# A weight pool allocated ahead of a small pool: the same program with one group of tiles at another on-chip address

## The chip, the cores and the metric

One NeuronCore of one Trainium2 chip runs the whole program. The metric is the device time of one launch in microseconds; before the change it is 2462.82 us, the median of three runs (2461.47 to 2467.37).

## What is computed

The reference sends 512 tokens of width 1024 through two attention layers and then through two layers of a second kind, all in float32. Cut to the parts that hold the matmuls:

```python
h = rms_norm(x, g_pre)                       # attention layer, twice
... = split_cols(h @ w_in)                   # queries, keys, values, gates, z
mixed = concat([o_a, o_b, o_c]) * silu(z)
x = x + rms_norm(mixed @ w_out, g_post)

swiglu(x) = (silu(x @ w_gate) * (x @ w_up)) @ w_down   # D_FF = 2816
# second part, twice: swiglu and layer norm, a token mixer (w_in_2, w_out_2) and layer norm, swiglu and layer norm
```

## The kernel before, in words

Tokens and features lie 128 to a tile. Each float32 product of an activation with a weight is made of three matmuls: both operands are split into a high part (rounded to the format that TensorE takes at one pass, `float32r`) and a low part (the remainder), and high x high, high x low and low x high are added in PSUM (`mm3`). The split activations are `xH`, `xL` (the layer's input, transposed), `oH`, `oL` (sums of quarters of the input) and `hH`, `hL` (the hidden layer of the feed-forward block). The split weights are `wH`, `wL`.

A weight is loaded by DMA from the SP queue into a tile `raw` (or `rs`, in the feed-forward block's first half), ScalarE writes `wH` (L185) and VectorE `wL` (L186). There are two buffers `raw` and five pairs `wH`, `wL`, each 4096 bytes per partition, all in the pool `w`. `raw`, `wH` and `wL` hold every large weight matrix of the program in turn.

Each matmul loads a stationary operand of 128 columns into the array and then streams a moving operand past it. Which of the two is the weight differs by the stage. In the first half of a feed-forward block (`Seven`, a seven-product scheme), and in the columns computed transposed, the weight is stationary and the activation moves, 256 or 512 columns at a time. In the second half of the feed-forward block and in the output projections, the activation is stationary and the weight moves, 512 columns at a time. The order of TensorE's instructions is written out by hand in most stages (`order(True)`).

Pools are stacked in the order in which they are opened: `const`, `persist` (`x`, `xH`, `xL`, each 16384 bytes per partition), `small`, `w`, and behind these the pools of the two program halves. Every buffer takes its bytes per partition, rounded up to 32. The pool `small` holds statistics of rows; its buffers sum to 4672 bytes: six each of `ss`, `nm`, `rec`, `mx`, `nms`, `den`, `lbm`, `mv`, `hss` at 32 bytes, six each of `rv`, `rr`, `st` at 64, one `thc` and two `hd` at 512, one `hT` at 256. The pool `w` takes 12 x 4096 = 49152 bytes. The second program half begins with a tile `pad` of 416 bytes (L996), behind which stand a tile of 32 bytes, the rows of the layer norms (4096 bytes each), and then `hL`, `hH`, `oH`, `oL`, `rs` of the feed-forward block, all multiples of 512 bytes long.

In this text the residue of a tile is its address in a partition modulo 512 bytes, and r is the residue of `x`, `xH` and `xL`. Since 4672 = 9 x 512 + 64, the pool `w` has residue r + 64 in the kernel before. Since 64 + 416 + 32 = 512, the tiles `hH`, `hL`, `oH`, `oL` and `rs` have residue r. Rows of these tiles start at multiples of 512 bytes from the tile's start, so that a matmul's 128 columns, or its 256 or 512 columns, begin at the residue of the tile. The exception is the first group of attention weights (`attn_weights`, L382), whose parts for the successive slices of the contraction lie 332 columns (1328 bytes) apart.

Of the kernel before, what the change touches and what calls it, by code (L numbers as in the profile page):

```python
# [75 lines left out]
class Net:  # L76
# [51 lines left out]
    def setup(self):  # L128
        nc, es = self.nc, self.es
        cp = self.cp = self.pool(es, "const")  # L130
        self.ident = cp.tile([P, P], F32, name="ident")
        make_identity(nc, self.ident)
        self.nhalf = cp.tile([P, 16], F32, name="nhalf")
        nc.gpsimd.memset(self.nhalf, -0.5)
        warm = cp.tile([P, 1], F32, name="warm")
        nc.scalar.activation(warm, self.nhalf[:, 0:1], AF.Square)
        pp = self.pool(es, "persist")
        self.x = pp.tile([P, NT, D], F32, name="x")
        self.xH = pp.tile([P, KD, T], F32R, name="xH")
        self.xL = pp.tile([P, KD, T], F32R, name="xL")  # L140
        self.small = self.pool(es, "small", bufs=6)
        self.wp = self.pool(es, "w")
        self.banks = [self.pool(es, f"ps{i}", bufs=2, space=PSUM) for i in range(3)]
        self.psS, self.psv, self.psm = self.banks
        self.pst = self.pool(es, "pst", bufs=2, space=PSUM)
        self.n_raw, self.n_pair = 2, 5
# [1384 lines left out]
```

## Time and profile before

| | |
|---|---|
| median of three runs | 2462.82 us |
| the profiled execution | 2465.12 us |
| its span, first to last instruction | 2463.4 us |
| TensorE matmuls, busy | 2384.7 us (97%) |
| VectorE busy | 1766.4 us (72%) |
| ScalarE busy | 1008.7 us (41%) |
| mean granted TensorE clock | 0.993 |

The span is 1.7 us shorter than the execution's own time. A busy share says how long an engine had an instruction in flight; TensorE's matmuls are pipelined, so that a matmul may take 0.39 us from start to end while the next one starts 0.23 us after it. What a matmul costs in a row of matmuls is therefore the distance between two starts, here called the step, and not its duration. In the trace a matmul is named out<-moving,stationary.

### The profile page before, as it was taken

Reading aid. Unit: us, or ns where it says so; the run is one execution under the profiler, and the core shown is the slowest. Engines: PE = TensorE matmul, PEld = TensorE weight load, DVE = VectorE, ACT = ScalarE, POOL = GpSimd, SP = SyncE. Lnnn points to the kernel's source line nnn. Section 1 sums busy time; section 2 is a strip of 40 time slices with the busy share of each in tenths; the row PEclk is TensorE's granted clock in tenths of the full one; section 3 lists DMA queues with packets and bytes.
Section 4 is the critical chain, followed back from the end, with each engine's and each line's share of the span. In section 5 each row is a group of like instructions: output and inputs, shape, how many; then the busy total and the mean of one; then the engine's idle time right before and its main releaser. Section 6 shows DMA issues by size and latency. Waiting matters only on the chain.

```text
span 2463.4 us, 38376 instructions
## 1 busy us (share of the span) xinstructions
PE 2384.7 (97%) x15542; PEld 2124.6 (86%) x15542; DVE 1766.4 (72%) x3011; ACT 1008.7 (41%) x1524; POOL 124.8 (5%) x184
## 2 busy tenths in 40 slices
PE   7999999999799999999899999899999999899998
PEld 6878888788789898887789898889898887889897
DVE  4566565665879596575888687979597576979596
ACT  4444443453445352322345353445352222445351
POOL 2000010000000001012000000000001012000000
PEclk9999999999999999999999999999999999999999
DMA  6422142112433333323343333343323223343322
GB/s 182 111 58 86 52 109 52 48 61 69 133 116 103 103 86 88 119 66 95 94 123 104 103 95 120 94 128 112 95 78 115 83 70 111 90 118 111 101 78 85
DMA packets 221919, 236.98 MB, mean 96 GB/s; under 512 B 35584, under 2 KB 177728, under 8 KB 221230
## 3 DMA queue, kind: packets, MB, share of 16 engines
q1 hardware_dynamic: 214736, 215.75, 30.0%
q10 hardware_dynamic: 5150, 10.34, 1.3%
q0 software_dynamic: 1856, 8.44, 1.1%
q8 instruction: 122, 2.00, 0.3%
q14 instruction: 55, 0.45, 0.1%
HBM read 230.25 MB, written 4.24 MB: 95 GB/s over the span
## 4 chain that ended last, share of the span: by engine, by line
PE 83%; DVE 8%; DMA 4%; ACT 2%; issue 2%; POOL 1%; SPq 0%; DVEq 0%; ACTq 0%; POOLq 0%
PE bk L121 59%; PE mm L121 13%; PE pv L121 3%; PE bh L121 3%; PE S L121 3%; DVE wL L186 2%; PE tr L338 2%; DVE rs L1430 1%; DMA raw<-in_w_in_dram 1%; PE tr L220 1%; ACT wH L185 1%; DMA rs<-in_ffn_up_dram 1%; DMA raw<-in_ffn_up_dram 1%; DVE xL L222 0%; DVE x L1043 0%
## 5 line engine op out<-in xcount | busy, mean ns | idle before, releaser
L121 PE MATMUL bk<-xH,wH 128*128 128x256 f32 (+1 forms) x1664 | 485.3, 292 | 10.2 <-DVE G L1474 4.5
L121 PE MATMUL bk<-xL,wH 128*128 128x256 f32 (+1 forms) x1664 | 478.1, 287 | 3.2 <-DVE xL L222 3.2
L121 PE MATMUL bk<-xH,wL 128*128 128x256 f32 (+1 forms) x1664 | 478.9, 288 | 0.0
L185 ACT ACTIVATE wH<-rs 128x1024 fp32r<-128x1024 f32 (+1 forms) x320 | 314.9, 987 | 333.0 <-PE bk L121 270.4
L186 DVE TENSOR_TENSOR wL<-rs,wH 128x1024 fp32r<-128x1024 f32 (+1 forms) x320 | 360.2, 1129 | 99.1 <-ACT wH L185 98.9
L186 DVE TENSOR_TENSOR wL<-raw,wH 128x1024 fp32r<-128x1024 f32 (+1 forms) x198 | 242.2, 1224 | 185.3 <-ACT wH L185 178.3
L185 ACT ACTIVATE wH<-raw 128x1024 fp32r<-128x1024 f32 (+1 forms) x198 | 209.5, 1058 | 315.3 <-PE bk L121 154.2
L121 PEld LDWEIGHTS bk<-xH,wH 128*128 128x128 f32 x1664 | 315.3, 189 | 24.0 <-DVE G L1474 8.5
L121 PEld LDWEIGHTS bk<-xL,wH 128*128 128x128 f32 x1664 | 315.0, 189 | 10.8 <-DVE xL L222 4.0
L121 PEld LDWEIGHTS bk<-xH,wL 128*128 128x128 f32 x1664 | 314.7, 189 | 5.1
L121 PE MATMUL bk<-oH,wH 128*128 128x256 f32 x1056 | 294.7, 279 | 6.0 <-ACT oH L221 3.7
L121 PE MATMUL bk<-oL,wH 128*128 128x256 f32 x1056 | 293.7, 278 | 4.4 <-DVE oL L222 4.4
L121 PE MATMUL bk<-oH,wL 128*128 128x256 f32 x1056 | 293.0, 277 | 0.0
L121 PE MATMUL bk<-wH,hL 128*128 128x512 f32 x704 | 277.4, 394 | 0.0
L121 PE MATMUL bk<-wL,hH 128*128 128x512 f32 x704 | 276.0, 392 | 0.0
L121 PE MATMUL bk<-wH,hH 128*128 128x512 f32 x704 | 274.1, 389 | 0.0
L1430 DVE TENSOR_TENSOR rs<-rs 128x1024 f32<-128x1024 f32 (+1 forms) x192 | 217.1, 1134 | 13.8 <-DMA rs<-in_ffn_gate_dram 10.5
L121 PEld LDWEIGHTS bk<-oH,wH 128*128 128x128 f32 x1056 | 199.7, 189 | 8.3 <-ACT u L1479 3.1
L121 PEld LDWEIGHTS bk<-oL,wH 128*128 128x128 f32 x1056 | 199.4, 189 | 5.4 <-DVE oL L222 5.2
L121 PEld LDWEIGHTS bk<-oH,wL 128*128 128x128 f32 x1056 | 199.4, 189 | 0.0
L121 PEld LDWEIGHTS bk<-wL,hH 128*128 128x128 f32 x704 | 132.2, 188 | 29.6
L121 PEld LDWEIGHTS bk<-wH,hH 128*128 128x128 f32 x704 | 132.2, 188 | 28.2
(285 smaller groups left out, 4086.3 us busy)
## 6 DMA issues: line engine op xcount, KB each, us to landing
raw<-in_ffn_down_dram SPq DMA_DIRECT2D x88, 512.0 KB, 3.8
rs<-in_ffn_gate_dram SPq DMA_DIRECT2D x80, 512.0 KB, 4.6
rs<-in_ffn_up_dram SPq DMA_DIRECT2D x80, 512.0 KB, 4.1
raw<-in_w_in_dram SPq DMA_DIRECT2D x64, 512.0 KB, 3.7
raw<-in_w_out_dram SPq DMA_DIRECT2D x32, 512.0 KB, 3.7
raw<-in_w_in_dram SPq DMA_DIRECT2D x16, 256.0 KB, 3.6
w<-in_cmp_w_dram SPq DMA_DIRECT2D x8, 512.0 KB, 4.1
raw<-in_ffn_gate_dram SPq DMA_DIRECT2D x8, 512.0 KB, 4.7
```

Source lines behind the costliest of these rows:

```text
L121: return self.nc.tensor.matmul(out, lhsT=lhsT, rhs=rhs, start=start, stop=stop, **kw)
L185: nc.scalar.activation(H[:, :n], raw[:, :n], AF.Copy)
L186: nc.vector.tensor_tensor(out=L[:, :n], in0=raw[:, :n], in1=H[:, :n].bitcast(F32), op=ALU.subtract)
L220: nc.tensor.transpose(ps[:, k, :], src[:, k * P:(k + 1) * P], self.ident)
L338: nc.tensor.transpose(pT[:, j * P:(j + 1) * P], keep["p"][:, j * P:(j + 1) * P], self.ident)
L1430: self.nc.vector.tensor_tensor(out=raw[to][:, :n], in0=raw[a][:, :n], in1=raw[b][:, :n], op=op)
```

## The change

The line that opens the pool `w` moves one line up, ahead of the line that opens `small`. No instruction, wait, queue or order of instructions is named by it.

```diff
         self.xL = pp.tile([P, KD, T], F32R, name="xL")
+        self.wp = self.pool(es, "w")
         self.small = self.pool(es, "small", bufs=6)
-        self.wp = self.pool(es, "w")
```

By the sizes above, the pool `w` moves down by 4672 bytes, from residue r + 64 to residue r. The pool `small` moves up by 49152 = 96 x 512 bytes and keeps its residues. The two together take as much as before, so that all later pools keep their addresses.

## Rows read from the trace of the kernel before

**Rows 1.** The page: busy time of each engine, and the granted clock by slices.
```profile
PE 2384.7 (97%) x15542; PEld 2124.6 (86%) x15542; DVE 1766.4 (72%) x3011; ACT 1008.7 (41%) x1524; POOL 124.8 (5%) x184
PEclk9999999999999999999999999999999999999999
```

**Rows 2.** The page: the chain that ended last, by engine.
```profile
PE 83%; DVE 8%; DMA 4%; ACT 2%; issue 2%; POOL 1%; SPq 0%; DVEq 0%; ACTq 0%; POOLq 0%
```

**Rows 3.** Groups by form: tiles, shape, count | busy us, mean ns | idle before.
```profile
L121 PE MATMUL bk<-xH,wH 128*128 128x256 f32 x1536 | 434.8, 283 | 10.2 <-DVE G L1474 4.5 <-ACT xH L221 2.8 <-DVE h L1474 2.6
...
L121 PE MATMUL bk<-oH,wH 128*128 128x256 f32 x1056 | 294.7, 279 | 6.0 <-ACT oH L221 3.7 <-ACT u L1479 2.3
...
L121 PE MATMUL bk<-wH,hL 128*128 128x512 f32 x704 | 277.4, 394 | 0.0
L121 PE MATMUL bk<-wL,hH 128*128 128x512 f32 x704 | 276.0, 392 | 0.0
L121 PE MATMUL bk<-wH,hH 128*128 128x512 f32 x704 | 274.1, 389 | 0.0
...
L121 PE MATMUL mm<-wH,xH 128*128 128x512 f32 x256 | 107.6, 420 | 0.4 <-DVE th L590 0.4
L121 PE MATMUL bk<-wL,xH 128*128 128x512 f32 x256 | 103.1, 403 | 0.9 <-DVE wL L186 0.8
...
L121 PE MATMUL mm<-xL,wH 128*128 128x512 f32 x144 | 56.8, 394 | 0.0
...
L121 PE MATMUL bk<-xL,wH 128*128 128x512 f32 x128 | 50.5, 395 | 0.0
```

**Rows 4.** Stretches, TensorE alone: window, length, busy (matmuls), granted clock, DMA.
```profile
32.30:34.60 2.30, 2.30 (x12) 0.50 0.48 118
744.00:750.00 6.00, 6.00 (x55) 1.00 0.35 98
821.00:858.00 37.00, 37.00 (x164) 1.00 0.22 63
1008.00:1029.00 21.00, 21.00 (x92) 1.00 0.34 103
```

**Rows 5.** Timeline, 256 columns, at half clock, then full: start us, duration us, engine, tiles.
```profile
32.27 0.41 PE L121 MATMUL mm<-wL,xH 128*128 128x256 f32 x1
...
34.19 0.41 PE L121 MATMUL mm<-wL,xH 128*128 128x256 f32 x1
...
744.83 0.28 PE L121 MATMUL bk<-oL,wH 128*128 128x256 f32 x1
...
749.93 0.28 PE L121 MATMUL bk<-xL,wH 128*128 128x256 f32 x1
```

**Rows 6.** Timeline, feed-forward's second half, weight moving, 512 columns.
```profile
820.07 0.28 PE L121 MATMUL bk<-xH,wL 128*128 128x256 f32 x1
820.18 0.39 PE L121 MATMUL bk<-wH,hH 128*128 128x512 f32 x1
820.41 0.39 PE L121 MATMUL bk<-wL,hH 128*128 128x512 f32 x1
...
858.40 0.39 PE L121 MATMUL bk<-wH,hL 128*128 128x512 f32 x1
```

**Rows 7.** Timeline, 512 columns, activation moving.
```profile
1007.48 0.40 PE L121 MATMUL bk<-xL,wH 128*128 128x512 f32 x1
...
1029.42 0.39 PE L121 MATMUL bk<-xH,wL 128*128 128x512 f32 x1
```

**Rows 8.** Timeline, 256 columns, then 512 with the weight moving: another rhythm.
```profile
933.84 0.28 PE L121 MATMUL bk<-oH,wL 128*128 128x256 f32 x1
933.96 0.40 PE L121 MATMUL bk<-wH,hH 128*128 128x512 f32 x1
...
939.33 0.39 PE L121 MATMUL bk<-wH,hL 128*128 128x512 f32 x1
...
988.99 0.28 PE L121 MATMUL bk<-xL,wH 128*128 128x256 f32 x1
...
991.35 0.28 PE L121 MATMUL bk<-xH,wH 128*128 128x256 f32 x1
```

**Rows 9.** Timeline, first attention weights, 332 columns: first matmul of four successive slices.
```profile
37.14 0.31 PE L121 MATMUL mm<-wH,xH 128*128 128x332 f32 x1
...
37.58 0.31 PE L121 MATMUL mm<-wH,xH 128*128 128x332 f32 x1
...
38.03 0.32 PE L121 MATMUL mm<-wH,xH 128*128 128x332 f32 x1
...
38.49 0.31 PE L121 MATMUL mm<-wH,xH 128*128 128x332 f32 x1
```

**Rows 10.** VectorE by form, the split of a weight from two kinds of tile.
```profile
L186 DVE TENSOR_TENSOR wL<-rs,wH 128x1024 fp32r<-128x1024 f32 x264 | 322.3, 1222 | 90.9 <-ACT wH L185 90.6
L186 DVE TENSOR_TENSOR wL<-raw,wH 128x1024 fp32r<-128x1024 f32 x192 | 235.8, 1228 | 183.0 <-ACT wH L185 176.0 <-PE bh L121 3.1 <-PE tr L121 2.8
```

## The prediction

> **What bounds the kernel.** The page comes first: TensorE is busy for 97% of the span at the full granted clock, 2.4 GHz, in every slice, VectorE for 72% [rows 1]. The chain of waits agrees: 83% of it is TensorE, VectorE and the DMAs together hold 12% [rows 2]. The groups by form then say which matmuls these are [rows 3], and the stretches that TensorE's share there is complete: 6.00 of 6.00, 37.00 of 37.00 and 21.00 of 21.00 us busy in the three stretches that I read closely [rows 4]. So the end is set by how closely one matmul follows another, and a change of a few ns in that step comes through almost whole. The view that gives the step is the timeline: the distance of two starts, divided by the matmuls between them.
>
> Four steps matter. With 256 columns, the activation moving: 45 steps from 744.83 to 749.93 us, 5.10 / 45 = 113.3 ns [rows 5]. With 512 columns, the weight moving: 166 steps from 820.41 to 858.40, 228.9 ns [rows 6]. With 512 columns, the activation moving: 94 steps from 1007.48 to 1029.42, 233.4 ns [rows 7]. The same instructions have a second rhythm: 23 steps of the 512-column form with the weight moving in 5.37 us, 233.5 ns, and 20 steps of the 256-column form in 2.36 us, 118.0 ns [rows 8]. In each of these stretches the step hardly varies, so I read it as a rhythm into which a row of matmuls falls and in which it stays.
>
> None of these is the plain streaming time. In a stretch at a granted clock of 0.50, 1.2 GHz [rows 4], 256 columns step 1.92 us / 9 = 213.3 ns [rows 5], which is one column per cycle; at the full clock that would be 106.7 ns, against the 113.3 measured. Something takes 6.6 ns of each 256-column matmul and 15.6 to 20.1 of each 512-column one (213.3 subtracted). Each step also loads the next stationary operand while the moving one streams, so two reads run side by side. That addresses within 512 bytes can bear on this is shown by the attention weights of 332 columns: there the moving operand's residue goes r + 368, r + 160, r + 64 from slice to slice while the stationary one stays at r, and three matmuls take 0.44, 0.45 and 0.46 us [rows 9], 146.7 to 153.3 ns each at the same shape.
>
> **The change, part by part.** No instruction, DMA or wait is added, removed or moved. What moves is the address of `raw`, `wH` and `wL`, from residue r + 64 to r, by which moving and stationary operand of all large matmuls stand at the same residue. I go by who touches these tiles.
>
> VectorE and ScalarE: nothing. Splitting from `rs`, which has residue r while the weight tiles have r + 64, takes 1222 ns; from `raw`, where all operands share a residue, 1228 [rows 10]. Half a percent of 192 instructions of 1228 ns is 1.2 us either way, on an engine with 28% to spare.
>
> DMA writes into `raw`: nothing. Both addresses lie at the same place within 64 bytes, and a load lands while TensorE runs; the DMAs of the chain are 4% [rows 2], and I bound this at 2 us either way.
>
> TensorE, 256 columns with the activation moving (residue r) and the weight stationary: 3 x 1536 + 3 x 1056 = 7776 matmuls [rows 3]. The kernel before shows the coming combination once at the end of a row of them: the last 256-column matmul reads x at r while `hH`, also at r, is loaded. Its step is 820.18 - 820.07 = 0.11 us [rows 6], as its predecessors have; the same place at 933.84 has 0.12 us, in a row that was already in the 118 rhythm [rows 8]. There are 24 such places, 22 like the first and 2 like the second. So I take 0 for this part. Its ends are 118.0 ns, +4.7 x 7776 = +36.5 us, and the plain streaming time, -6.6 x 7776 = -51 us; the lower end has no row at the full clock and I give it no room.
>
> TensorE, 512 columns with the weight moving: the weight's residue goes from r + 64 to r, the stationary operand stays at r. This is 3 x 704 with `hH`, `hL` and 3 x 256 each for the mixer's (`bk`) and the attention layers' (`mm`) matmuls, 3648 in all [rows 3]. No row shows this pair of residues for 512 columns. The nearest is the row in which the moving operand already stands at r, the activation moving, and it steps 233.4 instead of 228.9 ns [rows 6, 7]. The second rhythm of the very instructions in question is the same 233.5 [rows 8]. I take 233.4: +4.5 x 3648 = +16.4 us. About a fifth of it I strike: the stretches that are already in the slow rhythm, and the first few matmuls of each stretch of 24, which haven't fallen into a rhythm; that leaves +13 us. Bounds: if all three of a triple ran like its shortest, 389 ns of duration instead of the mean of 389, 392 and 394 [rows 3], it is -2.7 x 3648 = -10 us; at 118/113.3 of today's step, it would be +9.5 x 3648 = +35 us.
>
> TensorE, 512 columns with the activation moving: 3 x (144 + 128) = 816 matmuls [rows 3], now at 233.4. They get the stationary weight at r. I take 0; if they fell to 228.9, -3.7 us. The 332-column matmuls and the rest are some 200 and can't move 2 us.
>
> Sum: 2465.1 + 13 = 2478 for the profiled execution; that execution is 2.3 us above the median of the three runs, so 2476 as a median. TensorE has nothing behind which it hides: where its row of matmuls becomes longer by 13 us, VectorE and ScalarE, which wait for it, only get more room.
>
> A rule that speaks against all this is in the Trainium skill, "SBUF — State Buffer", section "Who interferes with whom": TensorE has two read ports, one for the moving operand and one for the weight load, and never waits for anyone. "TensorE: Matmul & The Clock Gate", section "Back-to-back issue gap", gives N / 2.4 + 2.5 ns, which is 215.8 for 512 columns, at any address. By both, the sum would be zero. The trace does not agree with the gap: 228.9 and 233.4 ns, and 146.7 to 153.3 for one shape at three residues [rows 6, 7, 9].
>
> **The rivals.** *No change.* The step is set by the rhythm alone, whichever address it comes from, and both reads go through ports of their own. For it speaks that one shape at one pair of residues has two rhythms [rows 6, 8], against it that three residues give three steps [rows 9]. Time: 2463, and within 2457 to 2469. The rule cited above would give the same.
>
> *Faster.* With both reads at one residue they start in the same place and run apart from there, since the moving one goes faster; if what they lose today is lost in a crossing later on, the crossing would go. Place: the 512-column rows. Price: -10 us from the shortest of each triple and -3.7 us from the rows with the activation moving, so 2449; it decides where more than half of the 3648 fall into the shorter rhythm. Against it: in the 24 places with both at r the step did not become shorter [rows 6].
>
> *The 256-column rows lose their rhythm.* One place at the end of a row shows that the 113.3 step exists with both at r, not that a row falls into it from its first matmuls. If they settle at 118.0 [rows 8], this costs 36.5 us: 2499 alone, 2512 with the forecast's 13.
>
> **How the numbers follow.** The forecast has 0.44, no change 0.25, faster 0.17, the lost rhythm 0.14. The forecast alone would be 2470 to 2482. The range goes from 2452, which cuts off the lower half of the faster case, to 2498, which cuts off most of the last. A measurement of this kernel tells about 0.3%, 7.4 us, from no change: slower by more than that are the forecast and the lost rhythm, 0.58; faster 0.17; within it 0.25.
>
> **What would show it.** Right: in the profile after, the stretches of the feed-forward's second half step 233 ns, the groups `bk<-wH,hH`, `bk<-wL,hH` and `bk<-wH,hL` have durations near 396 on the mean instead of 392, and the 256-column groups stay at 277 to 283. Wrong: 512-column steps at 229 or below, or 256-column steps away from 113.3; then the reason, that the residue of the moving operand decides, has failed, whatever the total. A changed duration of the VectorE split would show a part that I set to nothing.

## The result, and the profile after

The changed kernel takes 2482.21 us (median of six runs, 2479.61 to 2484.5), the kernel before, run beside it, 2465.62 us (six runs, 2461.47 to 2470.39). The ratio is 1.0066, 95% interval 1.005 to 1.0081; the medians differ by 16.6 us. The forecast was 2476 us and slower; the direction came true, but its reason did not hold, as the steps show.

The page of the changed kernel, busy time of each engine, and the chain that ended last:

```profile
PE 2413.7 (97%) x15542; PEld 2169.5 (87%) x15542; DVE 1769.2 (71%) x3011; ACT 1007.8 (41%) x1524; POOL 126.4 (5%) x184
...
PE 88%; DVE 6%; DMA 2%; ACT 2%; issue 1%; POOL 1%; SPq 0%; ACTq 0%; DVEq 0%; POOLq 0%
```

Against [rows 1] TensorE is busy 29.0 us longer, with the same 15542 matmuls; VectorE and ScalarE moved by less than 3 us. The span grew by only 2480.0 - 2463.4 = 16.6 us, so TensorE's idle time fell from 78.7 to 66.3 us (span less busy). The chain says the same: TensorE's share rose from 83 to 88%, VectorE's and the DMAs' fell from 12 to 8% [rows 2].

The groups by form of the changed kernel (tiles, shape, count | busy us, mean ns | idle before):

```profile
L121 PE MATMUL bk<-xH,wH 128*128 128x256 f32 x1536 | 441.3, 287 | 4.7 <-ACT xH L221 2.7 <-DVE h L1474 2.0
...
L121 PE MATMUL bk<-oH,wH 128*128 128x256 f32 x1056 | 301.3, 285 | 3.7 <-ACT oH L221 3.4
...
L121 PE MATMUL bk<-wH,hH 128*128 128x512 f32 x704 | 274.7, 390 | 0.0
L121 PE MATMUL bk<-wL,hH 128*128 128x512 f32 x704 | 274.2, 389 | 0.0
L121 PE MATMUL bk<-wH,hL 128*128 128x512 f32 x704 | 273.9, 389 | 0.0
```

Beside [rows 3] the 512-column triple went from 389, 392 and 394 to 390, 389 and 389 ns, so it became shorter; the two 256-column groups shown became 4 and 6 ns longer. The idle time in front of these two fell, from 10.2 to 4.7 and from 6.0 to 3.7 us.

The timeline of the changed kernel gives the steps (start us, duration us, engine, tiles; the first and last matmul of a row):

```profile
743.56 0.28 PE L121 MATMUL bk<-oH,wH 128*128 128x256 f32 x1
...
749.92 0.28 PE L121 MATMUL bk<-oH,wL 128*128 128x256 f32 x1
...
820.18 0.28 PE L121 MATMUL bk<-xH,wL 128*128 128x256 f32 x1
820.30 0.40 PE L121 MATMUL bk<-wH,hH 128*128 128x512 f32 x1
...
858.18 0.39 PE L121 MATMUL bk<-wH,hL 128*128 128x512 f32 x1
...
1009.15 0.40 PE L121 MATMUL bk<-xH,wH 128*128 128x512 f32 x1
...
1030.71 0.40 PE L121 MATMUL bk<-xH,wL 128*128 128x512 f32 x1
```

256 columns, activation moving: 53 steps in 6.36 us, 120.0 ns, where [rows 5] had 113.3. 512 columns, weight moving: 167 steps in 37.88 us, 226.8 ns, where [rows 6] had 228.9. 512 columns, activation moving: 95 steps in 21.56 us, 226.9 ns, where [rows 7] had 233.4. The granted clock of the changed kernel is the full one in the first two of these stretches, as it was in [rows 4]:

```profile
744.00:750.00 6.00, 6.00 (x52) 1.00 0.27 87
821.00:858.00 37.00, 37.00 (x165) 1.00 0.21 67
```

The same over the whole trace, each start's distance to the next by class. "Clean" is the mean over the steps that hold no wait (under 130 ns for 256 columns, under 245 for 512); the sum takes all:

| class (moving operand) | matmuls | clean ns, before, after | sum us, before, after |
|---|---|---|---|
| 256 columns, `xH`, `xL` | 4608 | 114.0, 119.9 | 574.3, 586.6 |
| 256 columns, `oH`, `oL` | 3168 | 113.7, 120.0 | 372.6, 389.3 |
| 512, weight, `hH`/`hL` stationary | 2111 | 229.0, 227.0 | 484.5, 479.8 |
| 512, weight, mixer (`bk`) | 768 | 230.0, 228.3 | 189.6, 187.5 |
| 512, weight, attention (`mm`) | 768 | 230.4, 229.4 | 185.4, 184.9 |
| 512, activation (`mm`, `bk`) | 816 | 232.4 and 233.3, 230.0 and 227.4 | 199.8, 196.8 |

The 256-column classes add 29.0 us, the 512-column classes give back 10.3, and the rest of the kernel gives about 2; the sum over all steps is 16.9 us, the change of the span within 0.3.

### The profile page after: what moved, and what is told of

Read it like the earlier page. It is cut to its first block, busy times and chain, and to the rows that moved or that the text cites. A ratio compares the mean times of both kernels' runs of the same rounds, so it can differ in the third digit from the quotient of the medians.

```text
span 2480.0 us, 38376 instructions
## 1 busy us (share of the span) xinstructions
PE 2413.7 (97%) x15542; PEld 2169.5 (87%) x15542; DVE 1769.2 (71%) x3011; ACT 1007.8 (41%) x1524; POOL 126.4 (5%) x184
## 4 chain that ended last, share of the span: by engine, by line
PE 88%; DVE 6%; DMA 2%; ACT 2%; issue 1%; POOL 1%; SPq 0%; ACTq 0%; DVEq 0%; POOLq 0%
PE bk L121 64%; PE mm L121 12%; PE pv L121 3%; PE bh L121 3%; PE S L121 3%; PE tr L338 1%; PE tr L220 1%; DVE wL L186 1%; ACT wH L185 1%; DMA raw<-in_w_in_dram 1%; DMA raw<-in_ffn_up_dram 1%; DVE rs L1430 0%; POOL rr L212 0%; DVE xL L222 0%; DMA raw<-in_w_out_dram 0%
## 5 line engine op out<-in xcount | busy, mean ns | idle before, releaser
L121 PE MATMUL bk<-xH,wH 128*128 128x256 f32 (+1 forms) x1664 | 491.2, 295 | 4.7 <-ACT xH L221 2.7
L121 PE MATMUL bk<-xL,wH 128*128 128x256 f32 (+1 forms) x1664 | 487.4, 293 | 3.1 <-DVE xL L222 3.1
L121 PE MATMUL bk<-xH,wL 128*128 128x256 f32 (+1 forms) x1664 | 488.2, 293 | 0.0
L186 DVE TENSOR_TENSOR wL<-rs,wH 128x1024 fp32r<-128x1024 f32 (+1 forms) x320 | 359.7, 1128 | 118.9 <-ACT wH L185 117.8
L121 PEld LDWEIGHTS bk<-xH,wH 128*128 128x128 f32 x1664 | 321.4, 193 | 12.1 <-ACT xH L221 3.7
L121 PEld LDWEIGHTS bk<-xL,wH 128*128 128x128 f32 x1664 | 321.3, 193 | 9.9 <-DVE xL L222 3.8
L121 PEld LDWEIGHTS bk<-xH,wL 128*128 128x128 f32 x1664 | 321.1, 193 | 4.4
L121 PE MATMUL bk<-oH,wH 128*128 128x256 f32 x1056 | 301.3, 285 | 3.7 <-ACT oH L221 3.4
L121 PE MATMUL bk<-oL,wH 128*128 128x256 f32 x1056 | 300.6, 285 | 3.9 <-DVE oL L222 3.9
L121 PE MATMUL bk<-oH,wL 128*128 128x256 f32 x1056 | 299.8, 284 | 0.0
L121 PEld LDWEIGHTS bk<-wH,hL 128*128 128x128 f32 x704 | 132.1, 188 | 27.6
```

The costliest lines, as they stand in the source:

```text
L121: return self.nc.tensor.matmul(out, lhsT=lhsT, rhs=rhs, start=start, stop=stop, **kw)
L186: nc.vector.tensor_tensor(out=L[:, :n], in0=raw[:, :n], in1=H[:, :n].bitcast(F32), op=ALU.subtract)
```

## Experiments

From here on D is the address of the moving operand less that of the stationary one, in bytes, taken modulo 256 (why 256, at the run with 256 bytes). Before, D is +64 where the weight moves and -64 where the activation moves; after, it is 0 for both. Theory A: the step follows from D. Rivals: the address of the weights itself (theory B in the expectations), or where an operand starts within its 64 bytes (theory D there, not the difference D).

**The changed kernel, all large tiles 64 bytes further.** The weights stand at their residue of before, r + 64, and all differences are those of after.

```diff
+        gap = cp.tile([P, 16], F32, name="gap")
+        nc.gpsimd.memset(gap, 0.0)
         pp = self.pool(es, "persist")
```

> The changed kernel with 64 bytes more ahead of the pool of x: every tile of the program moves up by 64 bytes, so that the weights stand where they stood in the kernel before (r + 64) and x, o and h stand there too; the difference of their residues stays 0. Theory A, the difference between the residues of the moving and the stationary operand decides: as the changed kernel, ratio 1.0066 (1.005 to 1.008), 256-column steps 120 ns, 512-column steps 227. Theory B, the weights' own address within 512 bytes decides: as the kernel before, ratio 1.000 within 0.002, 113.3 and 229 ns.

Measured 2485.58 us, ratio 1.0067 (1.0052 to 1.0083), as the change itself. Its timeline, a row of 256 and one of 512 columns:

```profile
738.23 0.28 PE L121 MATMUL bk<-xH,wH 128*128 128x256 f32 x1
...
799.90 0.28 PE L121 MATMUL bk<-xL,wH 128*128 128x256 f32 x1
...
824.32 0.40 PE L121 MATMUL bk<-wH,hH 128*128 128x512 f32 x1
...
862.20 0.39 PE L121 MATMUL bk<-wH,hL 128*128 128x512 f32 x1
```

514 steps of 120.0 ns and 167 of 226.8, the steps of the changed kernel: the weights' own address is not what decides.

**The kernel before, only `hH` and `hL` moved by 64 bytes.** This sets D to 0 for the feed-forward's second half alone.

```diff
+            self.pool(es, "g0").tile([P, 16], F32, name="g0")
             hp = self.pool(es, "h")
+            self.pool(es, "g1").tile([P, 112], F32, name="g1")
             tp = self.pool(es, "ht")
```

> The kernel before, with hH and hL alone moved from r to r + 64, where the weights stand; x, o and the weights stay. So only the feed-forward's second half has equal residues. Theory A: its 512-column steps fall from 229.0 to 227.0 ns, 2111 of them, -4 us, and the 256-column steps stay at 113 to 114; ratio 0.998 (0.9965 to 1.000). Theory B, by which the weights' own address decides: nothing changes, ratio 1.000, steps 229 and 113.3. Theory C, the forecast's, that the moving operand's residue decides: as B.

Measured 2466.64 us, ratio 0.9993 (0.9983 to 1.0004). Its timeline, two rows of 256 columns and one of 512:

```profile
735.55 0.28 PE L121 MATMUL bk<-xH,wH 128*128 128x256 f32 x1
...
755.34 0.36 PE L121 MATMUL bk<-xH,wH 128*128 128x256 f32 x1
...
774.84 0.28 PE L121 MATMUL bk<-xL,wH 128*128 128x256 f32 x1
...
793.67 0.28 PE L121 MATMUL bk<-xH,wL 128*128 128x256 f32 x1
...
819.06 0.39 PE L121 MATMUL bk<-wH,hH 128*128 128x512 f32 x1
...
856.91 0.39 PE L121 MATMUL bk<-wH,hL 128*128 128x512 f32 x1
```

The 512-column steps are 226.6 ns (167 steps), so D = 0 makes this row shorter by itself, 5.2 us in the sum (484.5 to 479.3). The 256-column rows, whose addresses were not touched, stay in the two rhythms of before, 117.8 (168 steps) and 113.4 ns (166), but more of them take the longer one: the clean mean with `xH`, `xL` is 115.4 instead of 114.0. That ate the gain (6.3 us more in the two 256-column classes), so the part of theory A's expectation on the 256-column steps and on the total did not come true. Theory B and theory C, the forecast's, by which the moving operand's residue decides, expected no change in the 512-column steps, since the weights stayed; both fell.

**The changed kernel, only `hH` and `hL` moved by -64 bytes.** The same two lines, with 112 ahead and 16 behind.

> The changed kernel with hH and hL alone moved down by 64 bytes within 512, so that the feed-forward's second half has the weights 64 above h again, as in the kernel before, while all the 256-column matmuls keep equal residues. Theory A: 512-column steps with h back at 229, 256-column steps stay at 120; ratio to the kernel before 1.008 (1.0065 to 1.010), that is the changed kernel plus 4 us. Theory B and C: as the changed kernel, 1.0066, with the 512-column steps at 227.

Measured 2489.7 us, ratio 1.0079 (1.0058 to 1.01). Its timeline:

```profile
738.19 0.28 PE L121 MATMUL bk<-xH,wH 128*128 128x256 f32 x1
...
799.99 0.28 PE L121 MATMUL bk<-xH,wL 128*128 128x256 f32 x1
...
824.32 0.39 PE L121 MATMUL bk<-wH,hH 128*128 128x512 f32 x1
...
862.54 0.39 PE L121 MATMUL bk<-wH,hL 128*128 128x512 f32 x1
```

D = +64 again in the second half: 228.9 ns, the step of before, while the 256-column rows keep 120.0 on the mean. The two effects are separate, and the 256-column one makes the kernel slower.

**The kernel before, all large tiles 32 bytes further.** The gap of the first experiment with 8 in place of 16: every operand starts elsewhere in its 64 bytes, the differences stay.

> The kernel before with 32 bytes more ahead of the pool of x: every tile moves up by 32 bytes and the differences stay; x and the weights now start at multiples of 64 bytes. Theory A as it stands, the difference alone decides: as before, ratio 1.000 within 0.003, steps 113.3 and 229. Theory D, the read goes by lines of 64 bytes, and a start within a line costs one more of them: 256 columns touch 16 lines instead of 17 and 512 columns 32 instead of 33, 6.7 ns less for each of 12,000 matmuls, -60 us or more, ratio 0.97 to 0.98.

Measured 2467.7 us, ratio 0.9994 (0.9984 to 1.0003). Its timeline:

```profile
736.30 0.28 PE L121 MATMUL bk<-xH,wH 128*128 128x256 f32 x1
...
755.26 0.28 PE L121 MATMUL bk<-xH,wL 128*128 128x256 f32 x1
...
819.25 0.39 PE L121 MATMUL bk<-wH,hH 128*128 128x512 f32 x1
...
857.47 0.39 PE L121 MATMUL bk<-wH,hL 128*128 128x512 f32 x1
```

113.5 and 228.9 ns, the steps of before; the theory of the 64-byte line fell.

**The weights at other distances.** In the next five only the pool `w` moves against all activations, by a tile in front of it that `pad` gives back. For 128 bytes:

```diff
+        gap = self.pool(es, "gap").tile([P, 16], F32, name="gap")
+        nc.gpsimd.memset(gap, 0.0)
         self.wp = self.pool(es, "w")
...
-        pad = self.pool(es, "pad").tile([P, 104], F32, name="pad")
+        pad = self.pool(es, "pad").tile([P, 88], F32, name="pad")
```

For 256 and 448 the gap has 48 and 96 in place of 16, for 96 it has 8; for 32 it has 8, in the changed kernel. Each ran once, the first three beside a run of the kernel before of 2471.01 us, the last two beside one of 2466.92; the steps carry the argument here, not the totals.

At 128 bytes:

> The kernel before with 64 bytes more ahead of the weights' pool (and 64 fewer in the pad of the second half, so that x, o and h keep their residue r): the weights stand at r + 128. Theory A1, only equal residues are special: steps as in the kernel before, 256 columns 113.3 or 118, 512 columns 229 with the weight moving and 233 with the activation moving; ratio 1.000 within 0.004. Theory A2, each difference has steps of its own: 256 columns between 107 and 120 and 512 between 220 and 240, others than at 64 and at 0 by over 1 ns, ratio between 0.98 and 1.02.

2502.75 us. Its timeline:

```profile
760.90 0.28 PE L121 MATMUL bk<-xL,wH 128*128 128x256 f32 x1
...
799.95 0.28 PE L121 MATMUL bk<-xH,wH 128*128 128x256 f32 x1
...
826.19 0.39 PE L121 MATMUL bk<-wH,hH 128*128 128x512 f32 x1
...
843.84 0.40 PE L121 MATMUL bk<-wL,hH 128*128 128x512 f32 x1
```

118.7 ns (329 steps) and 232.2 ns (76 steps): both forms are longer than before. Not all rows here are alike. The one from 2368.02 us on, 647 steps, keeps 120.0 ns, and with the activation moving one row of 512 columns takes 233.4 and a later one 232.3. So at D = 128, as at -64, one distance has more than one rhythm. Theory A1, by which only equal residues are special, fell here; A2, by which each difference has steps of its own, stands.

At 256 bytes:

> The same with the weights at r + 256, half way round the 512 bytes. Theory A1: as the kernel before, steps 113.3 or 118, 229, 233, ratio 1.000 within 0.004. Theory A2: other steps; if what counts is where in the row of columns the two reads cross, both operands change places without effect here, and 512 columns with the weight moving and with the activation moving have one and the same step, within 1 ns.

2484.55 us. Its timeline:

```profile
735.48 0.28 PE L121 MATMUL bk<-xH,wH 128*128 128x256 f32 x1
...
799.91 0.28 PE L121 MATMUL bk<-xH,wH 128*128 128x256 f32 x1
...
821.57 0.40 PE L121 MATMUL bk<-wH,hH 128*128 128x512 f32 x1
...
859.45 0.39 PE L121 MATMUL bk<-wH,hL 128*128 128x512 f32 x1
```

120.0 (537 steps) and 226.8 ns, the steps of the changed kernel within 0.3 ns in each class of the table. So 256 bytes do what 0 does, and the period is not 512; it is taken as 256 here. The one other pair of distances 256 apart, +128 (weight moving) and -128 (activation moving) in the run before, is alike too: 232.2, and 232.3 or 233.4. `small` stands where it stood in the kernel before, so its move is not the cause of the change either.

At 448 bytes, which is -64:

> The same with the weights at r + 448, that is 64 below x, o and h. Theory A2: the difference with its sign counts, so that the two forms of 512 columns change places: 233 ns with the weight moving, 229 with the activation moving, against 229 and 233 in the kernel before; the 256-column step is new, between 107 and 120 ns. Theory A1: all as in the kernel before, 113.3 or 118, 229, 233, ratio 1.000 within 0.004.

2489.06 us. Its timeline, rows of 256 columns, of 512 with the weight moving, and of 512 with the activation moving:

```profile
737.56 0.28 PE L121 MATMUL bk<-xH,wH 128*128 128x256 f32 x1
...
757.35 0.35 PE L121 MATMUL bk<-xH,wH 128*128 128x256 f32 x1
...
822.48 0.39 PE L121 MATMUL bk<-wH,hH 128*128 128x512 f32 x1
...
861.45 0.40 PE L121 MATMUL bk<-wH,hL 128*128 128x512 f32 x1
...
1012.11 0.40 PE L121 MATMUL bk<-xH,wH 128*128 128x512 f32 x1
...
1033.87 0.39 PE L121 MATMUL bk<-xH,wL 128*128 128x512 f32 x1
```

The two 512-column forms have changed places: 233.4 ns with the weight moving, 229.1 with the activation moving, against 228.9 and 233.4 before. So it is the signed difference, and not which tile moves. The 256-column step, now at D = +64, is 117.8 in most rows; 36 of 648 groups of twelve steps keep 113 to 114.

At 96 and at 32 bytes:

> The kernel before with the weights at r + 96, x, o and h at r. Theory A2 with a period of 256 bytes (0 and 256 have given the same steps, 64 and 448 have changed places), the time being smooth between the differences tried: between those at 64 and 128, 256 columns 113 to 119 ns, 512 with the weight moving 229 to 232, ratio 1.000 to 1.013. If the differences that are odd multiples of 32 are a class of their own, less is lost where the two reads keep half a line apart: 256 columns under 113, ratio under 0.99.

> The weights at r + 32, x, o and h at r. Smooth between 0 and 64: 256 columns 113 to 120 ns, 512 columns 227 to 229, ratio 0.998 to 1.007. A class of its own: as for r + 96, 256 columns under 113, ratio under 0.99.

2500.36 and 2492.0 us. The timeline at 96 bytes, a row of 256 columns:

```profile
759.40 0.28 PE L121 MATMUL bk<-xL,wH 128*128 128x256 f32 x1
...
799.15 0.32 PE L121 MATMUL bk<-xH,wH 128*128 128x256 f32 x1
```

118.7 ns (335 steps), and 233.4 with 512 columns and the weight moving; at 32 bytes the same two rows give 118.3 and 233.3. With 512 columns neither lies between its neighbours (226.8 at 0, 228.9 at +64, 232.2 at 128), so this step doesn't run smoothly with D. Neither idea of these expectations came true: with 512 columns the step isn't smooth between the distances tried, and the odd multiples of 32 are no class in which less is lost. All steps that long rows showed:

| D | 512 columns, ns | 256 columns, activation moving, ns |
|---|---|---|
| 0 | 226.6 to 226.9 | 120.0 |
| +64 | 228.9 and 229.1, seldom 233.5 [rows 8] | 117.8, seldom 113.3 |
| -64 | 233.4 | 113.3 or 118 |
| +32, -32 | 233.3, 233.5 | -, 118.3 |
| +96, -96 | 233.4, 234.2 | -, 118.7 |
| 128 | 232.2 to 233.4 | 118.7 or 120.0 |

The best difference for 512 columns, 0, is the worst for 256, with 128 beside it in a part of the rows.

**Is the choice between 113 and 118 ns one of the addresses?** The kernel before and the kernel with `hH`, `hL` moved were run and profiled once more.

> The kernel before, unchanged, profiled a second time (a comment at the end of the file is all that differs). Theory A1, the 256-column steps settle on 113.3 or on 118 ns per stretch, and which one is not set by the addresses: the 512-column classes repeat within 0.3 ns (229.0, 230.0, 230.4, 232.4, 233.3), the 256-column mean with activations moving lies elsewhere between 113.3 and 118 ns than the 114.0 of the first profile, by 0.3 ns or more, and stretches at 113.3 and at 118 fall in other places. Rival A2, addresses and program fix the rhythm of each stretch: 114.0 within 0.1 ns and the same stretches at 118. Both: ratio 1.000 within 0.002.

Measured 2467.94 us, ratio 0.9996 (0.9987 to 1.0006). The classes with 512 columns repeat within 0.1 ns; with 256 columns the clean mean is 114.6 instead of 114.0. Two rows of its timeline:

```profile
877.02 0.28 PE L121 MATMUL bk<-xL,wH 128*128 128x256 f32 x1
...
896.68 0.31 PE L121 MATMUL bk<-xH,wH 128*128 128x256 f32 x1
...
916.54 0.28 PE L121 MATMUL bk<-xL,wH 128*128 128x256 f32 x1
...
932.65 0.28 PE L121 MATMUL bk<-oH,wL 128*128 128x256 f32 x1
```

and the same two in the first profile of the kernel before (the second one ends at 933.84 [rows 8]):

```profile
878.11 0.28 PE L121 MATMUL bk<-xL,wH 128*128 128x256 f32 x1
...
896.92 0.28 PE L121 MATMUL bk<-xH,wL 128*128 128x256 f32 x1
...
917.12 0.28 PE L121 MATMUL bk<-xL,wH 128*128 128x256 f32 x1
```

The first of them runs at 117.7 ns in one execution (167 steps) and at 113.3 in the other (166); the second at 113.5 and at 117.7 (142 steps each). The same program at the same addresses takes either rhythm. It is not on record whether both profiles come from one chip.

> The kernel before with only the hidden activations (hH, hL) moved by 64 bytes, profiled a second time. Theory A1 (rhythm of the 256-column steps not set by the addresses): steps over the hidden activations 226.8 ns again, the 256-column mean differs from the 115.4 ns of its first profile by 0.3 ns or more, and the ratio to the kernel before follows it: about 0.998 (4.2 us of 2463) if the mean is near 114.0, about 1.000 if near 115.4 or over. Rival A2: 115.4 ns within 0.1 again and the same stretches at 118, ratio 0.9993.

Measured 2466.99 us, ratio 0.9998 (0.9982 to 1.0014). The steps over `hH`, `hL` are 226.8 again, and the 256-column mean is 115.5 after 115.4. Of 648 groups of twelve such matmuls 263 had a mean over 116 ns in its first profile and 287 in its second, 214 of them the same; for the kernel before it was 50 and 143, of which 20 the same, and 159 in the kernel with all tiles 32 bytes further, where every difference is that of before. So chance isn't all, and what theory A1 expected (a mean 0.3 ns or more away from 115.4) did not come true: with the shorter 512-column rows, more of the 256-column rows take 118, twice out of twice and largely in the same places. What decides it at the start of a row stays open. This kernel saves 5.2 us in one class and loses about as much in the other; it does not beat the kernel before. A version with D = -64 for all 256-column and D = 0 for all 512-column matmuls would need the input activations at two addresses 64 bytes apart at different times; that was not tried.

## Why the prediction was right or wrong

**What bounds the kernel** held: a few ns in the step of one kind of matmul moved the end by 16 us. But "comes through almost whole" did not. The clean 256-column steps cost 4441 x 5.9 + 3117 x 6.3 = 45.8 us, and 29.0 of them are in the class's sum. The other 16.8 us went in the steps that hold a wait: TensorE came later to a place where it had waited for VectorE or ScalarE (`G`, `h`, `xH`, `oH`, `u` in front of these groups). Its idle time bears this out: it fell by 12.4 us in all, by 8.4 of them in front of the 256-column groups (23.8 to 15.4 us). The windows read for 100% busy time were right for themselves; the idle 78.7 us lay elsewhere, and I had not set them against a cost spread over the whole kernel.

**VectorE, ScalarE, DMAs at nothing** held, as far as the profile shows it: ScalarE is busy 1007.8 us against 1008.7, and the DMAs' share of the chain fell from 4 to 2%. The split on VectorE in the changed kernel, by form:

```profile
L186 DVE TENSOR_TENSOR wL<-rs,wH 128x1024 fp32r<-128x1024 f32 x264 | 321.9, 1222 | 108.7 <-ACT wH L185 107.7
L186 DVE TENSOR_TENSOR wL<-raw,wH 128x1024 fp32r<-128x1024 f32 x192 | 235.3, 1226 | 178.8 <-ACT wH L185 171.0 <-PE bh L121 3.0 <-PE tr L121 2.5
```

1222 and 1226 ns, against 1222 and 1228 [rows 10].

**256 columns, "So I take 0"**, is the step that failed and that decides the sign. I drew it from one place per row, a single step of 0.11 us with both operands at one residue [rows 6]. The same place in the changed kernel has the same pair of residues, `x` and `hH` at r, and steps 820.30 - 820.18 = 0.12 us: it goes with the row that it ends, in either kernel, and not with its own pair. The changed kernel also has a single short step, from 858.41 to 858.52 us, at the start of a row that then keeps 120.0 ns. One step at the edge of a row says nothing of the step that the row keeps. The bound of 118.0 from the other rhythm [rows 8] was also too low; D = 0 has a step of its own.

**512 columns, weight moving, "I take 233.4"**, failed in sign. I read the moving operand's own residue as the cause and took the row with the activation moving as nearest. The run with 448 bytes shows that row for what it was, D = -64. At D = 0 the step is 226.8, and the class lost 7.3 us (4.7 + 2.1 + 0.5) where I had put +13. The lower bound, -10 us from the shortest of a triple, was near.

**512 columns, activation moving** went to 226.9 where I took 0 and bounded it by 228.9: -3.0 us against -3.7.

So the total, 6 us over the forecast (2.8 of them because the kernel before measured 2465.62 us beside it and not 2462.82), came out near by luck, from two errors of opposite sign: +29.0 where I had 0, -10.3 where I had +13. What the prediction named as the sign of its failure, 512-column steps at 229 or below and 256-column steps away from 113.3, is what the profile shows, both at once. The rivals were each half right: *faster* in the 512-column rows, *the lost rhythm* in the 256-column rows, at 5.9 to 6.3 ns in place of 4.7, of which waits took over a third. I had priced them as alternatives; they are one cause, D = 0, seen at two lengths.

*No change* fell: 512 columns take 226.6 to 234.2 ns by the distance of the two operands. By the Trainium skill, "SBUF — State Buffer", section "Who interferes with whom", TensorE's two read ports are independent and it never waits for anyone. These steps do not agree with that independence; what it is inside TensorE or the memory that makes one read bear on the other, no run here shows.

## What to carry to other kernels

Where a matmul streams one operand while the next stationary one is loaded, the difference of the two addresses modulo 256 bytes belongs to the things that a layout sets, and its sign with it: try 0 for 512 columns and -64 (moving below stationary) for 256, one shape at a time, and expect one shift to help one and hurt the other. Only `float32r` matmuls that each load a new weight of 128 columns were measured here. Read the step over a whole row and not at its ends. Before a change in the step is multiplied by the number of matmuls, set it against the waits that those matmuls lead up to: here they took over a third of it.

## What the runs showed of the hardware that was not expected

The step of a row depends on D, the same at 0 and 256 bytes and not evenly in sign: over the distances tried 512 columns range over 7.6 ns and 256 columns over 6.7, up to 4.7 of which one distance can show by itself (113.3 or 118 at -64).

Four of the rows' steps are multiples of 6.67 ns, 16 cycles at 2.4 GHz: 113.3 is 17 of them, 120.0 is 18, 226.7 is 34, 233.3 is 35. The means of the longest rows at 117.8 and 228.9 are 17 2/3 and 34 1/3 of them. All of these are means of a row. Single steps can hold still (120 ns each in the first row of the changed kernel) or go round: 225 to 232 ns in the row of 228.9, 231 to 236 in that of 233.4 (the rows of [rows 6] and [rows 7]), so that "hardly varies" in the prediction holds for the mean and not for each step. Why the rows fall on this grid is not shown here.

Part of the spread between executions goes with the clock. The ten executions of the kernel with `hH`, `hL` moved, the second time, run from 2459.02 us at a mean granted clock of 0.996 to 2474.25 us at 0.990. One window of the changed kernel shows a place where clock is lost (length, busy time of TensorE and then of the weight loads, VectorE, ScalarE and GpSimd, granted clock, DMA):

```profile
600.00:650.00 50.00, 40.35 (x240) 35.92 (x239) 37.72 (x65) 20.37 (x33) 2.40 (x5) 0.91 0.44 137
```

At the change from attention to feed-forward TensorE is idle for 9.65 of 50 us, and the granted clock of that stretch is 0.91, so part of it was at 1.2 GHz.
